# A two-block transformer on one core: where the experts' side work stands, and how the routing's slots are counted

## The chip, the cores and the metric

The kernel runs on one core of one Trainium2 chip. The metric is device time in microseconds of one execution; the median of several runs is compared. The engines' names are those of the profile: PE is TensorE (the matmuls), PEld its weight loads, DVE VectorE, ACT ScalarE, POOL GpSimd, SP the engine that issues most transfers.

## The reference

512 tokens of width 1024 go through two layers of a first block (four branches, a mixture of experts, a gated embedding) and two layers of a second one (three attentions). All is float32. The change touches the norms and the mixture of experts:

```python
def rms_norm(x, g):
    y = xf * lax.rsqrt(jnp.mean(xf * xf, axis=-1, keepdims=True) + EPS)

def expert_choice_moe(h, w_router, w_gate_e, w_up_e, w_down_e):
    cap = EC_CAPACITY * s // N_EXPERTS                      # 64 tokens for each of 16 experts
    affinity = jax.nn.softmax((h @ w_router).astype(jnp.float32), axis=-1)
    top_aff, idx = lax.top_k(jnp.swapaxes(affinity, 1, 2), cap)
    xe = h[bidx, idx]
    hid = silu(xe @ w_gate_e) * (xe @ w_up_e)               # 64 x 1024 by 1024 x 1024, per expert
    ye = hid @ w_down_e
    return jnp.zeros_like(h).at[bidx, idx].add(ye * top_aff[..., None])
```

Each expert chooses its 64 tokens, so every expert has the same amount of work, and its three matrices (4 MB each) are read once a layer.

## The kernel before, in words

The state `x` lies feature-major: eight tiles `x[kt]` of 128 features by 512 tokens. Products with float32 weights are done in two ways. Most are three matmuls of split values (`mm3`, a high and a low part). The experts' are plain float32 matmuls, which the trace shows as two records each.

`mean_sq` (L286) makes the mean of squares of `x` per token: ScalarE squares the eight tiles, VectorE adds them up one after the other (`sqa`), and four matmuls with a column of 1/1024 turn the sum into one number per token (`ms`). Eight places use it with one sum, one (the second block's first norm) with two.

`moe` (L1051) runs once in each of the first block's layers. **Routing:** the router's logits (`rlg`, `rlt`), the affinities `aff` (tokens on the partitions), and their transposes `aft` (16 experts on the partitions, 512 tokens along them). VectorE copies them to `w`, and eight times takes the eight largest and replaces them by -1. What is below zero then is the expert's choice. A scan along the tokens counts the chosen ones, times the mask; four transposes (`slt`) bring the counts back to tokens on the partitions, and `slot` holds for each token and expert the token's place 1 to 64, or 0. Meanwhile TensorE turns `x` (`h2t`) and computes the modulation of the second block (`ada`).

**Experts:** 16 experts in eight pairs (`pr`, counted from 0 to 7), 24 weight blocks of 1 MB a pair, fetched by SP in the order of use. A pool of buffers lets about ten blocks be ahead (`RING`). Expert `j` of a pair has 64 tokens; its matmuls have 64 weight columns and write 64 of the 128 partitions, `j` = 0 the lower half and `j` = 1 the upper one, each with its own weight block:

```python
for k2 in range(4):
    ts = [take() for j in range(2)]
    for k in range(2):
        for fh in range(2):
            for j in range(2):
                self.mat(two[fh][j * 64:j * 64 + 64], e[:, j * 64:j * 64 + 64], ts[j](k, fh), ...)
    step()
```

This is one step, eight matmuls or 16 records. The gate product has four steps and the up product four (`eg`), then come `sg` = silu of the gate, `hd` = `sg` times up, the transposes `hdt` and their copies `ht`, for the two halves `fh` of the width, and the down product with four steps (`ey`).

**Side work** comes from a list, `side`, one entry after each step, and what is left after the last one. Its entries: `scatter`, which adds a finished pair's results to one tile of `x` (two matmuls of 128x512 into `sct`, then an add on VectorE), eight for each pair, done during the next; `turned`, which transposes the pair's one-hot columns (`oht`) and picks the chosen affinities (`asl`); `gather`, which collects the tokens of four later experts (16 matmuls of 128x256 into `xe`, evicted half by VectorE, half by ScalarE), four in pair 1 and two each in pairs 2 to 5 (`GATHER`). The next stage's products `late` (a turn, eight parts `pw` of six matmuls, a load, two splits) come one after each step from pair 6 on, beside the list. All of the side work writes banks of the pool `at`, of which there are two.

The program only says what depends on what and in which order it was written; the framework lays out each engine's instructions. It goes by program order as a priority, and takes a later instruction where an earlier one isn't ready by its own estimate. So an engine's order in the trace need not be the program's: a gather can stand in two pieces around matmuls of the experts.

Of the kernel before, what the change touches and what calls it, by code (L numbers as in the profile page):

```python
# [10 lines left out]
FT = mybir.dt.float32  # L11
FR = mybir.dt.float32r
AF = mybir.ActivationFunctionType
OP = mybir.AluOpType
# [4 lines left out]
KT = 8  # L19
NB = 4  # L20
P = 128
# [67 lines left out]
class Net:  # L89
# [195 lines left out]

    def mean_sq(self, gains=(None,), on=None):  # L286

        acc = [None] * len(gains)
        pool = self.tr if len(gains) == 1 else self.ae
        for kt in range(KT):  # L290
            for i, g in enumerate(gains):
                sq = pool("sq")
                if g is None:
                    self.act(sq, self.x[kt], AF.Square)
                else:
                    self.act(sq, self.x[kt], AF.Square, scale=g[:, kt:kt + 1])
                if acc[i] is None:
                    acc[i] = sq
                else:
                    nx = pool("sqa")  # L300
                    (on or self.nc.vector).tensor_tensor(nx, acc[i], sq, op=OP.add)
                    acc[i] = nx
        ps = self.at("ms")
        for i in range(len(gains)):
            for tb in range(NB):
                self.mat(ps[:, i * NB + tb:i * NB + tb + 1], acc[i][:, tb * P:tb * P + P], self.inv1024)
        return [ps[:, i * NB:i * NB + NB] for i in range(len(gains))]

    def rms_cols(self, on=None):
# [741 lines left out]
    def moe(self, l, fill, late):  # L1051

        nc, ap = self.nc, self.ap
# [6 lines left out]
        def load():  # L1060
            to = plan.pop(0) if plan else "wst"
            src, k2 = order.pop(0)

            src = src.rearrange("(c p k) n -> c p k n", p=P, k=2)[k2]
            if to in ("fm", "tr", "ae"):
                t = [getattr(self, to)("we") for _ in range(4)]
                for k in range(2):
                    for h in range(2):
                        nc.sync.dma_start(t[k * 2 + h], src[:, k, h * S:h * S + S])
                ready.append(lambda k, h: t[k * 2 + h])  # L1070
            elif to == "wh":
                t = [self.sb.tile([P, 1024], FT, name="we" + y, tag=y, bufs=2) for y in ("wh", "wl")]
                for k in range(2):
                    nc.sync.dma_start(t[k], src[:, k])
                ready.append(lambda k, h: t[k][:, h * S:h * S + S])
            else:
                if to == "pt":
                    t = self.pt("we").rearrange("p a b -> p (a b)").rearrange("p (k n) -> p k n", k=2)
                elif to == "x":
                    if not half:  # L1080
                        for y in ("xh", "xl"):
                            big = self.sb.tile([P, 2, 2, D], FT, name="we" + y, tag=y, bufs=1)
                            half.extend((big[:, 0], big[:, 1]))
                    t = half.pop(0)
                else:
                    t = self.sb.tile([P, 2048], FT, name="wst", tag="wst", bufs=NW).rearrange("p (k n) -> p k n", k=2)
                nc.sync.dma_start(t, src)
                ready.append(lambda k, h: t[:, k, h * S:h * S + S])
# [46 lines left out]
        at = self.at("aft")  # L1135
        for tb in range(NB):
            self.tp(at[:16, tb * P:tb * P + P], afv[:, tb])
        w, cs = self.ae("rw"), self.ae("rcs")
        nc.vector.tensor_copy(w[:16], at[:16])
        for r in range(8):  # L1140
            m8 = self.sm("m8", 8)
            nc.vector.max(m8[:16], w[:16])
            nc.vector.match_replace(w[:16], m8[:16], w[:16], -1.0)
        ms = w
        self.ts(ms[:16], w[:16], 0.0, OP.is_lt)
        nc.vector.tensor_tensor_scan(cs[:16], ms[:16], ms[:16], 0.0, op0=OP.add, op1=OP.bypass)
        self.tt(cs[:16], cs[:16], ms[:16], OP.mult)

        hh = self.sb.tile([P, NB, 2, S], FR, name="h2h", tag="xl", bufs=1)
        hl = self.sb.tile([P, NB, 2, S], FR, name="h2l", tag="xh", bufs=1)  # L1150
        for hf in range(2):
            for tb in range(NB):
                ps = self.lgp("h2t")
# [6 lines left out]
        fill()  # L1160
        for _ in range(2):
            load()
        st = self.at("slt")
        for tb in range(NB):
            self.tp(st[:, tb * 16:tb * 16 + 16], cs[:16, tb * P:tb * P + P])
        slot = self.sb.tile([P, 64], FT, name="slot", tag="slot", bufs=1)
        nc.vector.tensor_copy(slot, st[:, :64])

        oh = [self.pt("oh%d" % hx, FR) for hx in range(2)]

# [28 lines left out]
        def turned(pr, out):  # L1199

            hx, cols = pr // 4, slice(pr % 4 * P, pr % 4 * P + P)
            ps = self.at("oht")
            for tb in range(NB):
                self.tp(ps[:, tb * P:tb * P + P], oh[hx][:, tb, cols].bitcast(FT))
            oht = self.ae("oht", FR)
            self.act(oht, ps, AF.Copy)
            pa = self.at("asl")
            for tb in range(NB):
                self.mat(pa[:, :2], oh[hx][:, tb, cols].bitcast(FT), afv[:, tb, pr * 2:pr * 2 + 2], start=tb == 0, stop=tb == NB - 1)
            asl = self.sm("asl", 1)  # L1210
            for j in range(2):
                nc.vector.tensor_copy(asl[j * 64:j * 64 + 64], pa[j * 64:j * 64 + 64, j:j + 1])
            out.extend((oht, asl))
# [5 lines left out]
            self.mat(ps, yl[:, c], oht, start=False, stop=True)  # L1219
            self.tt(self.x[i], self.x[i], ps, OP.add)  # L1220

        side = []

        def step():
            if side:
                side.pop(0)()
            if late and pr >= 6:
                late.pop(0)()
        xs, nxt = [], []
        onehot(0)  # L1230
        for pr in range(8):
            tn = []
            g4, part = GATHER.get(pr, (0, ()))
            if part and part[0] == 0:
                onehot(g4)
                nxt = []
            side.append(lambda pr=pr, tn=tn: turned(pr, tn))
            for d2 in part:
                side.append(lambda g4=g4, d2=d2, nx=nxt: gather(g4, d2, nx))
            xc = pr % 2 * P  # L1240
            pss = []
            for pool in (self.mm, self.lgp):
                two = [pool("eg%d" % i) for i in range(2)]
                for k2 in range(4):
                    ts = [take() for j in range(2)]
                    if pr == 0 and pool == self.mm:
                        gather(0, k2, xs)
                    for k in range(2):
                        kt = k2 * 2 + k
                        e = xs[kt // 2][:, kt % 2 * 256 + xc:kt % 2 * 256 + xc + P]  # L1250
                        for fh in range(2):
                            for j in range(2):
                                self.mat(two[fh][j * 64:j * 64 + 64], e[:, j * 64:j * 64 + 64],
                                         ts[j](k, fh), start=kt == 0, stop=kt == KT - 1)
                    step()
                pss.append(two)
            hts = []
            for fh in range(2):
                sg, hd = self.ae("sg"), self.ae("hd")
                self.act(sg, pss[0][fh], AF.Silu)  # L1260
                self.tt(hd, sg, pss[1][fh], OP.mult)
                pt = self.at("hdt")
                for k in range(4):
                    self.tp(pt[:, k * P:k * P + P], hd[:, k // 2 * 256 + k % 2:k // 2 * 256 + 256:2])
                ht = self.ae("ht")
                self.copy(ht, pt)
                hts.append(ht)
            py = [self.mm("ey%d" % i) for i in range(2)]
# [3 lines that stand above are left out]
                    ft = k2 * 2 + k  # L1272
                    for dh in range(2):
                        for j in range(2):
                            self.mat(py[dh][j * 64:j * 64 + 64], hts[ft // 4][:, ft % 4 * P + j * 64:ft % 4 * P + j * 64 + 64],
                                     ts[j](k, dh), start=ft == 0, stop=ft == KT - 1)
                step()
            while side:
                step()
            for dh in range(2):  # L1280
                yh, yl = self.tr("yh", FR), self.tr("yl", FR)
                self.split(yh, yl, py[dh], tn[1])
                for d in range(4):
                    side.append(lambda i=dh * 4 + d, yh=yh, yl=yl, oht=tn[0]: scatter(i, yh, yl, oht))
            if pr % 2:
                xs = nxt
        while side or late:
            step()

    def ple_pre(self, l):  # L1290

# [473 lines left out]
```

## Time and profile before

| | us |
|---|---|
| median of 3 runs | 3566.06 |
| lowest and highest | 3564.95, 3567.53 |
| the profiled execution, its own time | 3565.2 |
| span of the profile | 3563.5 |
| PE busy | 3430.4 |
| DVE busy | 1806.6 |
| ACT busy | 1133.5 |

The span goes from the first to the last instruction. A matmul counts as busy from its start to its modelled end, and neighbours overlap, so busy time does not tell how densely the array works; that is read from the distance of starts in the timeline. In the tables by stretch the columns are: from and to, the length, then for PE, PEld, DVE, ACT and POOL the busy time with the number of instructions, and last the granted clock of PE, the busy share of the transfer engines and the GB/s they moved. In a timeline the first two numbers are the start and the length; in square brackets stands the idle time before and what ended it.

The transfers moved 655.97 MB, 181 GB/s over the span, most of it in the two stages with the experts.

### The profile page before, as it was taken

Reading aid. Unit: us, or ns where it says so; the run is one execution under the profiler, and the core shown is the slowest. Engines: PE = TensorE matmul, PEld = TensorE weight load, DVE = VectorE, ACT = ScalarE, POOL = GpSimd, SP = SyncE. Lnnn points to the kernel's source line nnn. Section 1 sums busy time; section 2 is a strip of 40 time slices with the busy share of each in tenths; the row PEclk is TensorE's granted clock in tenths of the full one; section 3 lists DMA queues with packets and bytes.
Section 4 is the critical chain, followed back from the end, with each engine's and each line's share of the span. In section 5 each row is a group of like instructions: output and inputs, shape, how many; then the busy total and the mean of one; then the engine's idle time right before and its main releaser. Section 6 shows DMA issues by size and latency. Waiting matters only on the chain. (4 is left out here: it accounts for less than half of the span.)

```text
span 3563.5 us, 42081 instructions
## 1 busy us (share of the span) xinstructions
PE 3430.4 (96%) x15961; PEld 2298.0 (64%) x15961; DVE 1806.6 (51%) x3533; ACT 1133.5 (32%) x2209; POOL 419.1 (12%) x646
## 2 busy tenths in 40 slices
PE   8999999999999999999999999899999999999998
PEld 7867774443437877776434436676678877676887
DVE  7567652111117776673111115697644459756344
ACT  4344641000104444562000113225433322544333
POOL 0110421000000120151000000330210013103000
PEclk9999999999999999999999999899999999999999
DMA  5233667999993233465999985231123332221322
GB/s 177 73 88 108 199 216 282 385 387 388 376 378 109 66 111 105 149 231 202 388 373 402 380 353 226 71 101 62 46 76 103 102 116 76 79 71 36 107 95 71
DMA packets 315437, 655.97 MB, mean 184 GB/s; under 512 B 31075, under 2 KB 208575, under 8 KB 280931
## 3 DMA queue, kind: packets, MB, share of 16 engines
q1 hardware_dynamic: 291968, 628.78, 48.1%
q0 software_dynamic: 8192, 15.22, 1.7%
q10 hardware_dynamic: 15075, 9.29, 0.9%
q8 instruction: 126, 2.06, 0.2%
q14 instruction: 76, 0.62, 0.1%
HBM read 629.59 MB, written 14.70 MB: 181 GB/s over the span
## 5 line engine op out<-in xcount | busy, mean ns | idle before, releaser
L153 PE MATMUL pj<-xh,wh 128*128 128x512 f32 x1808 | 728.1, 404 | 14.3 <-DVE gb L150 6.4
L153 PE MATMUL pj<-xh,wl 128*128 128x512 f32 (+1 forms) x1808 | 725.1, 402 | 10.7 <-DVE wl L142 10.7
L153 PE MATMUL pj<-xl,wh 128*128 128x512 f32 (+1 forms) x1808 | 724.8, 401 | 0.9 <-DVE xl L150 0.7
L132 ACT ACTIVATE wh<-wst 128x1024 fp32r<-128x1024 f32 (+2 forms) x368 | 339.0, 930 | 754.2 <-PE pj L153 570.0
L142 DVE TENSOR_TENSOR wl<-wst,wh 128x1024 fp32r<-128x1024 f32 (+2 forms) x368 | 413.4, 1126 | 308.1 <-ACT wh L132 307.6
L153 PEld LDWEIGHTS pj<-xh,wh 128*128 128x128 f32 x1808 | 342.0, 189 | 110.0 <-DVE gb L150 9.6
L153 PEld LDWEIGHTS pj<-xh,wl 128*128 128x128 f32 (+1 forms) x1808 | 342.0, 189 | 102.7 <-DVE wl L142 13.7
L153 PEld LDWEIGHTS pj<-xl,wh 128*128 128x128 f32 (+1 forms) x1808 | 341.9, 189 | 94.2 <-issue 12.8
L153 PE MATMUL eg<-wst,xe 128*64 128x512 f32 x1008 | 293.0, 596 | 0.0
L153 PE MATMUL eg<-we,xe 128*64 128x512 f32 x560 | 228.4, 596 | 0.0
L153 PEld LDWEIGHTS eg<-wst,xe 128*64 128x64 f32 x1008 | 94.6, 136 | 134.1 <-issue 125.5
L142 DVE TENSOR_TENSOR x<-x,sct 128x512 f32<-128x512 f32 x128 | 83.8, 684 | 187.6 <-PE sct L153 187.6
L142 DVE TENSOR_TENSOR hd<-sg,eg 128x512 f32<-128x512 f32 x32 | 21.9, 685 | 309.0 <-PE eg L153 242.8
L153 PE MATMUL ey<-wst,ht 128*64 128x512 f32 x512 | 161.1, 599 | 7.4 <-DVE ht L139 3.9
L272 POOL TENSOR_TENSOR rr<-msb,mhalf 128x4 f32<-128x4 f32 x9 | 9.2, 1021 | 1344.9 <-DVE msb L146 1344.9
L153 PE MATMUL pt<-wh,xh 128*128 128x256 f32 x512 | 145.9, 285 | 1.4 <-DVE ro L142 1.2
L153 PE MATMUL pt<-wl,xh 128*128 128x256 f32 x512 | 145.1, 283 | 0.0
L153 PE MATMUL pt<-wh,xl 128*128 128x256 f32 x512 | 145.0, 284 | 0.0
L132 ACT ACTIVATE e<-e,nm 128x512 f32<-128x512 f32 (+3 forms) x192 | 111.2, 581 | 70.9 <-DVE nm L146 70.4
L1391 POOL TENSOR_TENSOR wada<-wada 128x1024 f32<-128x1024 f32 (+1 forms) x48 | 101.8, 2121 | 131.5 <-ACT wada L132 129.6
L153 PE MATMUL ey<-we,ht 128*64 128x512 f32 x256 | 115.3, 597 | 1.5 <-DVE ht L139 0.8
L153 PEld LDWEIGHTS eg<-we,xe 128*64 128x64 f32 x560 | 68.2, 136 | 74.2 <-issue 65.2
(495 smaller groups left out, 5788.9 us busy)
## 6 DMA issues: line engine op xcount, KB each, us to landing
wst<-in_w_in_dram SPq DMA_DIRECT2D x90, 1024.0 KB, 5.3
wst<-in_w_exp_gate_dram SPq DMA_DIRECT2D x66, 1024.0 KB, 8.6
wst<-in_w_exp_down_dram SPq DMA_DIRECT2D x64, 1024.0 KB, 11.1
wst<-in_w_exp_up_dram SPq DMA_DIRECT2D x60, 1024.0 KB, 7.8
wst<-in_w_branch_gate_dram SPq DMA_DIRECT2D x32, 1024.0 KB, 5.6
wada<-in_w_ada_dram SPq DMA_DIRECT2D x24, 1024.0 KB, 5.2
we<-in_w_exp_up_dram SPq DMA_DIRECT2D x88, 256.0 KB, 7.1
we<-in_w_exp_down_dram SPq DMA_DIRECT2D x80, 256.0 KB, 9.1
```

The lines of the kernel that those rows point to most:

```text
L132: return self.nc.scalar.activation(out, in_, func, **kw)
L142: return self.nc.vector.tensor_tensor(out, a, b, op=op)
L153: return self.nc.tensor.matmul(out, lhsT, rhs, start=start, stop=stop, **kw)
L272: self.nc.gpsimd.tensor_tensor(r, ms, self.mhalf[:, :n], op=OP.pow)
L1391: nc.gpsimd.tensor_tensor(t[:, :k], t[:, :k], t[:, k:2 * k], op=OP.add)
```

## The change

- In `mean_sq` the last square is no longer added: the sum of the first seven and the eighth square both go through the four matmuls, which add up in the bank.
- In the routing VectorE takes the first maxima straight from the transposes' bank. What is left after the eight rounds is transposed at once; the mask is taken there (64 columns), and the count is four matmuls: one with a triangle of ones within each block of 128 tokens, three with all ones that add the blocks before. A product with the mask gives `slot`.
- The list `side` becomes two: `sc`, scatters two at a time, and `ga`, gathers. Scatters stand after the first and third step of the gate and up products; `late` after the second and fourth. A gather stands before each `hd` (two where the pair has four), one after the last step of the down product, and what is left after it. `turned` has a fixed place after the second step of the down product.

```diff
@@ -285,7 +285,7 @@
 
     def mean_sq(self, gains=(None,), on=None):
 
-        acc = [None] * len(gains)
+        acc, last = [None] * len(gains), []
         pool = self.tr if len(gains) == 1 else self.ae
         for kt in range(KT):
             for i, g in enumerate(gains):
@@ -294,16 +294,21 @@
                     self.act(sq, self.x[kt], AF.Square)
                 else:
                     self.act(sq, self.x[kt], AF.Square, scale=g[:, kt:kt + 1])
-                if acc[i] is None:
+                if kt == KT - 1:
+                    last.append(sq)
+                elif acc[i] is None:
                     acc[i] = sq
                 else:
                     nx = pool("sqa")
                     (on or self.nc.vector).tensor_tensor(nx, acc[i], sq, op=OP.add)
                     acc[i] = nx
+
         ps = self.at("ms")
-        for i in range(len(gains)):
-            for tb in range(NB):
-                self.mat(ps[:, i * NB + tb:i * NB + tb + 1], acc[i][:, tb * P:tb * P + P], self.inv1024)
+        for src in (acc, last):
+            for i in range(len(gains)):
+                for tb in range(NB):
+                    self.mat(ps[:, i * NB + tb:i * NB + tb + 1], src[i][:, tb * P:tb * P + P], self.inv1024,
+                             start=src is acc and i + tb == 0, stop=src is last, skip_group_check=True)
         return [ps[:, i * NB:i * NB + NB] for i in range(len(gains))]
 
     def rms_cols(self, on=None):
@@ -1135,16 +1140,13 @@
         at = self.at("aft")
         for tb in range(NB):
             self.tp(at[:16, tb * P:tb * P + P], afv[:, tb])
-        w, cs = self.ae("rw"), self.ae("rcs")
-        nc.vector.tensor_copy(w[:16], at[:16])
+        w = self.ae("rw")
+        src = at
         for r in range(8):
             m8 = self.sm("m8", 8)
-            nc.vector.max(m8[:16], w[:16])
-            nc.vector.match_replace(w[:16], m8[:16], w[:16], -1.0)
-        ms = w
-        self.ts(ms[:16], w[:16], 0.0, OP.is_lt)
-        nc.vector.tensor_tensor_scan(cs[:16], ms[:16], ms[:16], 0.0, op0=OP.add, op1=OP.bypass)
-        self.tt(cs[:16], cs[:16], ms[:16], OP.mult)
+            nc.vector.max(m8[:16], src[:16])
+            nc.vector.match_replace(w[:16], m8[:16], src[:16], -1.0)
+            src = w
 
         hh = self.sb.tile([P, NB, 2, S], FR, name="h2h", tag="xl", bufs=1)
         hl = self.sb.tile([P, NB, 2, S], FR, name="h2l", tag="xh", bufs=1)
@@ -1160,11 +1162,20 @@
         fill()
         for _ in range(2):
             load()
+
         st = self.at("slt")
         for tb in range(NB):
-            self.tp(st[:, tb * 16:tb * 16 + 16], cs[:16, tb * P:tb * P + P])
+            self.tp(st[:, tb * 16:tb * 16 + 16], w[:16, tb * P:tb * P + P])
+        ms = self.sb.tile([P, 64], FT, name="chosen", tag="chosen", bufs=1)
+        self.ts(ms, st[:, :64], 0.0, OP.is_lt)
+        cn = self.at("cnt")
+        self.mat(cn[:, :64], self.tri[:, 0], ms, start=True, stop=False, skip_group_check=True)
+        for tb in range(1, NB):
+            self.mat(cn[:, tb * 16:64].rearrange("p (b e) -> p b e", e=16), self.one.to_broadcast([P, P]),
+                     ms[:, None, tb * 16 - 16:tb * 16].to_broadcast([P, NB - tb, 16]), start=False, stop=tb == NB - 1,
+                     skip_group_check=True)
         slot = self.sb.tile([P, 64], FT, name="slot", tag="slot", bufs=1)
-        nc.vector.tensor_copy(slot, st[:, :64])
+        self.tt(slot, cn[:, :64], ms, OP.mult)
 
         oh = [self.pt("oh%d" % hx, FR) for hx in range(2)]
 
@@ -1219,12 +1230,16 @@
             self.mat(ps, yl[:, c], oht, start=False, stop=True)
             self.tt(self.x[i], self.x[i], ps, OP.add)
 
-        side = []
-
-        def step():
-            if side:
-                side.pop(0)()
-            if late and pr >= 6:
+
+
+        sc, ga = [], []
+
+        def step(kind):
+            if kind == 0 and sc:
+                sc.pop(0)()
+            elif kind == 1 and ga:
+                ga.pop(0)()
+            elif late and pr >= 6:
                 late.pop(0)()
         xs, nxt = [], []
         onehot(0)
@@ -1234,9 +1249,8 @@
             if part and part[0] == 0:
                 onehot(g4)
                 nxt = []
-            side.append(lambda pr=pr, tn=tn: turned(pr, tn))
             for d2 in part:
-                side.append(lambda g4=g4, d2=d2, nx=nxt: gather(g4, d2, nx))
+                ga.append(lambda g4=g4, d2=d2, nx=nxt: gather(g4, d2, nx))
             xc = pr % 2 * P
             pss = []
             for pool in (self.mm, self.lgp):
@@ -1252,12 +1266,15 @@
                             for j in range(2):
                                 self.mat(two[fh][j * 64:j * 64 + 64], e[:, j * 64:j * 64 + 64],
                                          ts[j](k, fh), start=kt == 0, stop=kt == KT - 1)
-                    step()
+                    step(k2 % 2 * 2)
                 pss.append(two)
             hts = []
             for fh in range(2):
                 sg, hd = self.ae("sg"), self.ae("hd")
                 self.act(sg, pss[0][fh], AF.Silu)
+                step(1)
+                if len(part) == 4:
+                    step(1)
                 self.tt(hd, sg, pss[1][fh], OP.mult)
                 pt = self.at("hdt")
                 for k in range(4):
@@ -1274,18 +1291,21 @@
                         for j in range(2):
                             self.mat(py[dh][j * 64:j * 64 + 64], hts[ft // 4][:, ft % 4 * P + j * 64:ft % 4 * P + j * 64 + 64],
                                      ts[j](k, dh), start=ft == 0, stop=ft == KT - 1)
-                step()
-            while side:
-                step()
+                if k2 == 1:
+                    turned(pr, tn)
+                elif k2 == 3:
+                    step(1)
+            while ga:
+                step(1)
             for dh in range(2):
                 yh, yl = self.tr("yh", FR), self.tr("yl", FR)
                 self.split(yh, yl, py[dh], tn[1])
-                for d in range(4):
-                    side.append(lambda i=dh * 4 + d, yh=yh, yl=yl, oht=tn[0]: scatter(i, yh, yl, oht))
+                for d in (0, 2):
+                    sc.append(lambda i=dh * 4 + d, yh=yh, yl=yl, oht=tn[0]: [scatter(i + j, yh, yl, oht) for j in range(2)])
             if pr % 2:
                 xs = nxt
-        while side or late:
-            step()
+        while sc or late:
+            step(0)
 
     def ple_pre(self, l):
 
```

## Rows read from the trace of the kernel before

**Rows 1.** The page's first part: busy time, share of the span, instructions.

```profile
PE 3430.4 (96%) x15961; PEld 2298.0 (64%) x15961; DVE 1806.6 (51%) x3533; ACT 1133.5 (32%) x2209; POOL 419.1 (12%) x646
```

**Rows 2.** Busy time of each engine over the first layer's experts.

```profile
556.56:1077.04 520.48, 506.31 (x2125) 217.02 (x2125) 88.67 (x150) 52.49 (x87) 0.31 (x1) 1.00 0.95 375
```

**Rows 3.** The same view for `eg` alone, twice, and for `ey` alone.

```profile
694.20:715.05 20.85, 20.85 (x96) 8.61 (x96) 0.69 (x1) 0.60 (x1) 1.00 0.99 389
...
556.56:1077.04 520.48, 258.20 (x1024) 92.51 (x1024) 11.00 (x16) 9.51 (x16) 1.00 0.95 375
...
556.56:1077.04 520.48, 141.53 (x512) 43.93 (x512) 11.90 (x16) 10.90 (x16) 1.00 0.95 375
```

**Rows 4.** Timeline of PE in pair 1: start, length, engine, what, count, idle before.

```profile
613.22 0.50 PE L153 MATMUL sct<-oht,yh 128*128 128x512 f32 x1
...
613.88 3.65 PE L153 MATMUL eg<-wst,xe 128*64 128x512 f32 x16
617.46 0.50 PE L153 MATMUL sct<-oht,yh 128*128 128x512 f32 x1
...
622.37 1.93 PE L153 MATMUL eg<-we,xe 128*64 128x512 f32 x4
...
628.57 0.40 PE L153 MATMUL sct<-oht,yh 128*128 128x512 f32 x1
628.80 0.39 PE L153 MATMUL sct<-oht,yl 128*128 128x512 f32 x1
```

**Rows 5.** Timeline of PE in pair 2, the start of the down product.

```profile
716.48 1.93 PE L153 MATMUL ey<-wst,ht 128*64 128x512 f32 x4 [0.69 <-ACT ht L137]
718.34 0.75 PE L157 MATMUL hdt<-ident,hd 128*128 128x128 f32 x4
718.92 0.60 PE L157 MATMUL oht<-ident,oh 128*128 128x128 f32 x4
...
720.85 3.65 PE L153 MATMUL ey<-wst,ht 128*64 128x512 f32 x12
...
724.67 0.28 PE L153 MATMUL xe<-oh,h2l 128*128 128x256 f32 x1
724.79 0.28 PE L153 MATMUL xe<-oh,h2h 128*128 128x256 f32 x1
```

**Rows 6.** Waits of PE: who was waited for, us in total, times, longest.

```profile
PE slt L157 <- DVE rcs L142: 13.9, 2, 6.9
...
PE ms L153 <- DVE sqa L301: 7.6, 2, 4.8
```

**Rows 7.** Down parts (five summed, the last pair's); gate and up parts (seven summed).

```profile
sum 139.26, PE 133.68 PEld 64.56 DVE 17.16 ACT 17.60 POOL 0.00; mean PE 26.74 PEld 12.91 DVE 3.43 ACT 3.52 POOL 0.00
...
1050.07:1069.74 19.67, 18.64 (x85) 8.16 (x84) 1.72 (x5) 2.37 (x4) 0.00 (x0) 1.00 1.04 399
...
sum 280.26, PE 275.25 PEld 104.56 DVE 54.98 ACT 16.62 POOL 0.31; mean PE 39.32 PEld 14.94 DVE 7.85 ACT 2.37 POOL 0.04
```

**Rows 8.** Stretches of the experts; the last two numbers: DMA share, GB/s.

```profile
640.00:655.00 15.00, 13.97 (x63) 6.11 (x61) 4.02 (x10) 1.68 (x3) 0.00 (x0) 1.00 1.02 423
...
609.00:936.00 327.00, 317.62 (x1335) 132.86 (x1332) 54.20 (x96) 24.59 (x44) 0.00 (x0) 1.00 0.99 388
```

**Rows 9.** Timeline of DVE in the routing.

```profile
535.09 0.68 DVE L1139 COPY rw<-aft 16x512 f32<-16x512 f32 x1 [0.78 <-PE aft L157]
...
547.74 0.76 DVE L146 TENSOR_SCALAR rw<-rw 16x512 f32<-16x512 f32 x1
548.54 1.21 DVE L1146 TENSOR_TENSOR_SCAN rcs<-rw 16x512 f32<-16x512 f32 x1
549.79 0.68 DVE L142 TENSOR_TENSOR rcs<-rcs,rw 16x512 f32<-16x512 f32 x1
551.23 0.22 DVE L1167 COPY slot<-slt 128x64 f32<-128x64 f32 x1 [0.76 <-PE slt L157]
```

**Rows 10.** Timeline of PE at the second block's second norm.

```profile
2895.63 1.02 PE L153 MATMUL ms<-inv,sqa 128*128 128x1 f32 x8 [2.74 <-DVE sqa L301]
```

## The prediction, made before the changed kernel ran

> **What bounds the kernel now.** First the head of the page: TensorE is busy for 3430.4 us, 96% of the span [rows 1]. So time comes off only where TensorE's own work gets shorter, or where it waits with everybody behind it. Next the stage table, cut where the experts' matmuls begin and end: one layer's experts take 520.5 us, TensorE is busy through 506 of it and the transfers run at 375 GB/s [rows 2]. The second layer shows the same pattern, so I work out one layer and double it.
>
> Then I asked what a busy TensorE does there. In an undisturbed run 96 records of the gate and up matmuls take 20.85 us, 0.217 each [rows 3]. A pair of experts has 128 such records (two products, 8 row blocks, two halves of the width, two experts, two records per matmul) and 64 more in its down product, so a layer has 1536, which at 0.217 would take 333 us. The trace has 258.2 for `eg` and 141.5 for `ey` [rows 3]: 66 us a layer are lost inside "busy". The timeline says to what [rows 4, 5]:
> - Going out of the half-width matmuls and back. One step of 16 records with its scatter takes 4.24 us (613.22 to 617.46); 16 x 0.217 and two scatter matmuls at 0.23 (628.57 to 628.80) are 3.93. A break costs 0.31.
> - A step cut in two. A run of 4 records lasts 1.86 us to the next instruction (716.48 to 718.34), 0.465 a record: twice the undisturbed time, so I read it as one expert's half of the columns working alone. Its other 12 need 3.58 (720.85 to the gather that follows it, whose second record is at 724.67), as much as a whole undisturbed step (613.88 to 617.46). Each cut costs 1.86, on top of the break. The cuts lie where side work was taken in: a run of 4, transposes and `turned`, a run of 12, then a gather [rows 5].
>
> Last, the wait at the routing: TensorE stands still for 13.9 us in two waits until VectorE has the slots [rows 6].
>
> **The change, part by part.**
>
> *Gathers out of the down product.* Five pairs a layer gather for later ones (one pair four times, four pairs twice). Their down parts, from the first transpose of `hd` to the next pair, take 139.3 us together [rows 7]. Without side work but for the one `turned` in the middle, such a part is 64 x 0.217 = 13.9, two groups of four transposes at 0.58 (718.34 to 718.92) with a break, 1.5, and `turned` at no more than the 1.93 from 718.92 to 720.85. A gather is 16 records at 0.12 (724.67 to 724.79) and some 0.2 of entry, 2.1 [rows 5]. That gives 21.5 with two gathers and 25.7 with four, 111.7 for the five: 27.6 less. In this the 0.69 that `ey` waits for the copy of `ht` is gone as well [rows 5], since a gather fills it. What hides what: the gathers run while ScalarE and VectorE make `sg`, `hd` and `ht`. Behind them wait the transposes, which need one of the two `at` banks, so where two gathers stand together the first one's eviction must come ahead of them; with one gather the other bank is free. The bounds are 0 (the cuts come back elsewhere) and 27.6. I take all of it, since a down part with hardly any gather in it is short already: the last pair's takes 19.7 [rows 7].
>
> *Scatters two at a time, on every second step.* The gate and up parts of the seven pairs that scatter take 280.3 us [rows 7], with the next stage's `late` work in one of them. In program order each would be 128 x 0.217 = 27.8 and four runs of two scatters (4 x 0.23 + 0.31 = 1.23): 32.7, 229 for seven. The `late` work, eight parts of six matmuls at 0.23 with a break each, is some 14 of the rest: up to 37 to win. But the instructions don't stand in program order today: eight scatters that the program spreads over eight steps are done in the first five or six of their pair, and cut steps on their way, as at 622.37 [rows 4]. Where a scatter is taken early whenever a weight block isn't counted on yet, a new place in the program hardly moves it: bound below 0. The row nearest is that one, so I take 8 of 37.
>
> *Weights.* A layer's experts are 16 x 3 matrices of 4.19 MB, 201.3 MB. In 520.5 - 27.6 - 8 = 485 us the same transfers mean 375 x 520.5 / 485 = 402 GB/s. Over five pairs the queue brings 388 with its engines 0.99 busy, and 423 in the best of some 15 us stretches [rows 8]. So faster matmuls come close to what the transfers give, and what is late next is a weight block. I charge 4 us a layer; the bounds are 0 and, at 388 throughout, 375 x 520.5 / 388 = 503, which would leave 17 of the gain.
>
> On this the Trainium skill, "DMA: Bandwidth & Descriptors", section Specifications, speaks against the change: about 358 GB/s from HBM for one core. By that figure the layer's 188 MB that are left after 13 blocks fetched ahead take 524 us, and the experts gain nothing. The rows at 388 and 423 are already above it, so the measurement decides here.
>
> *`late` work.* Its last two items, the load of the next stage's first weights and their splits, move from the seventh pair to the eighth's up product, and SP sends the load behind more weight blocks. I cost it at nothing: the eighth's down part, 19.7 us [rows 7], lies ahead of its user. Without that cover it would be 1 MB at 388 GB/s, 2.7 us a layer. `turned` moves a few steps; its result is needed at the end of the down product, half a down part later. No instruction of POOL's queue moves.
>
> *Routing.* Off VectorE's chain go the copy 0.68, the compare 0.76, the scan 1.21 and the product 0.68: 3.33 [rows 9]. In come a compare and a product on 128x64 (0.22 each, one of them in place of the slot copy), one crossing to TensorE and back, and four small matmuls, eight records. The nearest is `ms`, eight records in 1.02 [rows 10]; these come after an idle stretch like it. With crossings of 0.1 to 0.4 the chain gets 1.0 to 2.0 shorter; I take 1.4 a layer, all of it gain, because TensorE idles there.
>
> *Norms.* The last add leaves the chain, an operation as long as the 0.68 of the same width in [rows 9], and eight more records come, as long as the eight of `ms`, 1.02 [rows 10]. Where TensorE waits for the add (twice, 7.6 us in all [rows 6]) and at the very end some 0.7 is gained, with the running sum's records standing in the wait; at the other six places the add was hidden and the records aren't, up to 1.0 lost each, against a chain that is 0.7 earlier. I take 0, bounds 4 either way.
>
> **Sum.** 27.6 + 8 - 4 = 31.6 a layer, 63 for two; routing 2.8; norms 0: 66 us. The profiled execution took 3565.2, so 3499; the median shown is 0.9 above it: 3500.
>
> **The rivals.**
> 1. *The transfers decide.* If 388 GB/s is what the mix of block sizes gives, each layer keeps 17.4 us: 3565.2 - 34.8 - 2.8 + 0.9 = 3528. For it: engines 0.99 busy at 388; against it: the stretch at 423. Chance 0.20. The page's 358 would be its extreme: only routing is left, 3563; with both rows above it I give that 0.01, inside rival 3.
> 2. *Program order holds everywhere.* 27.6 + 37 is more than the transfers allow: at 423 GB/s the stage can't be under 461 us, 59 less a layer: 3566 - 118 - 3 = 3445. Against it: today's order. Chance 0.12.
> 3. *The change doesn't do what it says.* The order on TensorE stays one of readiness, gathers fall into the down product as before, and only routing is left: 3563. For it: the cut steps of today. Against it: the gathers' new place is ahead of the transposes in program order, at a moment when TensorE has nothing else. Chance 0.09.
> 4. *Slower: more cut steps.* Longer runs of side work, some of it waiting from the start of a pair, get into the middle of steps. A cut and its break cost 2.2; the 66 us lost today are at most some 30 cuts a layer. From 14 more on (31.6 / 2.2) the change loses; with 21 more it is 14 us a layer: 3590. Chance 0.11.
>
> **How the numbers follow.** My forecast has 0.48, with a range of its own of 3475 to 3522 (the scatters' 0 to 20, the transfers' 0 to 10). A measurement of this kernel tells some 0.2%, 7 us, from no change. Faster: forecast, rivals 1 and 2, 0.80; same: rival 3, 0.09; slower: rival 4, 0.11. The range for 8 in 10 runs from rival 2 to the edge of "same": 3445 to 3558.
>
> **What would show it.** In the profile after: the five down parts together near 112, with `ey` in two runs of 32 and `xe` ahead of and between the `hdt` groups; `eg` and `ey` together well under 400 a layer; `sct` in runs of four, and fewer runs of 4 and 12; transfers above 400 GB/s over the same five pairs, and whether TensorE now names a weight transfer as what it waited for; the wait for `slt` near 5.5 each. I am wrong if `ey` still comes in runs of 4 and 12, or if waits for `we` and `wst` add up to tens of us.

## The result, and the profile after

The changed kernel takes 3520.62 us (median of 4 runs, 3519.08 to 3526.85), the kernel before beside it 3565.51: ratio 0.9877, 95% interval 0.986 to 0.9894, 44.9 us less. The forecast was 3500: right side and inside the range, but of the 66 us that it promised a third did not come.

The head of the page of the changed kernel [rows 1]:

```profile
PE 3408.0 (97%) x16057; PEld 2309.6 (66%) x16057; DVE 1794.9 (51%) x3517; ACT 1133.6 (32%) x2209; POOL 417.3 (12%) x646
```

TensorE is busy for 22.4 us less. The stage table over the experts of both layers, then the first layer's `eg` and its `ey` alone [rows 2, 3]:

```profile
560.91:1062.12 501.21, 491.64 (x2123) 215.62 (x2123) 88.42 (x150) 52.00 (x86) 0.31 (x1) 1.00 0.98 390
1643.85:2139.57 495.72, 486.69 (x2123) 215.06 (x2123) 87.69 (x150) 51.98 (x86) 0.00 (x0) 1.00 0.98 393
...
560.91:1062.12 501.21, 259.13 (x1024) 93.15 (x1024) 10.99 (x16) 9.52 (x16) 1.00 0.98 390
...
560.91:1062.12 501.21, 127.84 (x512) 42.54 (x512) 11.91 (x16) 10.89 (x16) 1.00 0.98 390
```

The first layer's experts are 19.3 us shorter, the second's 26.8 (522.5 before): 46 us, the whole gain. `ey` lost 13.7 of its busy time; `eg` nothing.

The parts of the first layer: the five down parts that had gathers in them, summed, then the gate and up parts of the seven pairs with scatters, summed [rows 7]:

```profile
sum 105.20, PE 104.44 PEld 50.47 DVE 14.16 ACT 14.74 POOL 0.00; mean PE 20.89 PEld 10.09 DVE 2.83 ACT 2.95 POOL 0.00
...
sum 293.85, PE 287.59 PEld 116.52 DVE 60.10 ACT 20.22 POOL 0.31; mean PE 41.08 PEld 16.65 DVE 8.59 ACT 2.89 POOL 0.04
```

The down parts are 34.1 us shorter, and the gate and up parts, forecast 8 shorter, are 13.6 longer. Neither can be read by itself. The parts meet at the first transpose of `hd`, and six of a layer's gathers, which the program now puts before the first `hd` of their pair, have crossed that border; the forecast counted all twelve in the down parts. Busy time of TensorE in the same seven gate and up parts: all instructions that use `xe`, which are the gathers and `eg`; `eg` alone; and, in the kernel before, `eg` alone, since no gather stood there:

```profile
sum 293.85, PE 242.55; mean PE 34.65
...
sum 293.85, PE 229.56; mean PE 32.79
...
sum 280.26, PE 228.71; mean PE 32.67
```

The six gathers are 13.0 of the 13.6 us. Counted as the forecast counts, the down parts gave 21.1 us of its 27.6, and the gate and up parts are 0.6 longer, with one part of `late`, some 1.7 us, gone from them (in pairs 6 and 7, where no gather is left, `late` takes the gathers' places too). Of runs of 4 records, the sign of a cut step, the first layer's `eg` has 16 before and 16 after, its `ey` 13 before and 1 after. So the cut steps left the down product and stayed as they were in the gate and up products. How they come about is in the timeline of TensorE in pair 3:

```profile
739.71 1.93 PE L153 MATMUL eg<-wewh,xe 128*64 128x512 f32 x4
741.57 0.73 PE L153 MATMUL sct<-oht,yl 128*128 128x512 f32 x2
742.84 0.50 PE L153 MATMUL sct<-oht,yh 128*128 128x512 f32 x1 [0.54 <-DVE x L142]
...
746.86 1.88 PE L153 MATMUL eg<-we,xe 128*64 128x512 f32 x4
748.67 0.50 PE L153 MATMUL sct<-oht,yh 128*128 128x512 f32 x1
...
750.17 0.49 PE L153 MATMUL sct<-oht,yh 128*128 128x512 f32 x1 [0.33 <-DVE x L142]
750.60 1.93 PE L153 MATMUL eg<-wst,xe 128*64 128x512 f32 x4
752.46 0.50 PE L153 MATMUL sct<-oht,yl 128*128 128x512 f32 x1
752.80 0.28 PE L153 MATMUL xe<-oh,h2h 128*128 128x256 f32 x1
...
753.97 3.65 PE L153 MATMUL eg<-wst,xe 128*64 128x512 f32 x12
```

A cut step begins with 4 records of one half alone (739.71, from `wewh`) and ends with 4 of the other half alone (746.86, from `we`), 1.9 us each, with scatters in between that the program puts after later steps. All eight scatters of the pair are through by 752.8; one of them, at 750.17 and 752.46, is itself cut in two. At 752.80 a gather, which stands behind the up product in the program, follows after 20 of the pair's 128 `eg` records, in the middle of a step. I read the runs of 4 as one half of a step that goes alone because the other's weight block isn't there yet in the framework's reckoning, with side work taken in its place; the halved transfers below test it.

The waits of TensorE at the two places [rows 6]:

```profile
PE slt L157 <- DVE rw L1148: 6.1, 2, 3.7
...
PE ms L153 <- ACT sq L132: 3.1, 2, 2.3
```

The routing's wait fell from 13.9 to 6.1. What stands behind it now (TensorE, from the routing to the first gather):

```profile
552.24 0.58 PE L157 MATMUL slt<-ident,rw 16*128 16x16 f32 x4 [3.75 <-DVE rw L1148]
553.23 0.66 PE L153 MATMUL cnt<-chosen,pc 128*128 128x64 f32 x2 [0.41 <-DVE chosen L146]
553.68 1.41 PE L153 MATMUL cnt<-chosen,one 128*128 128x48 f32 x6
555.95 0.55 PE L153 MATMUL xe<-oh,h2h 128*128 128x256 f32 x1 [0.87 <-DVE oh L1185]
```

From `slt` to the first gather it is 3.71 us, before 1.44: 2.27 of the 3.2 that the wait lost in this layer (6.94 before) are given back.

### The profile page after: what moved, and what is told of

The parts are those of the page before. It is cut to its first block, busy times and chain, and to the rows that moved or that the text cites. A ratio compares the mean times of both kernels' runs of the same rounds, so it can differ in the third digit from the quotient of the medians.

```text
span 3518.1 us, 42207 instructions
## 1 busy us (share of the span) xinstructions
PE 3408.0 (97%) x16057; PEld 2309.6 (66%) x16057; DVE 1794.9 (51%) x3517; ACT 1133.6 (32%) x2209; POOL 417.3 (12%) x646
## 5 line engine op out<-in xcount | busy, mean ns | idle before, releaser
L153 PEld LDWEIGHTS pj<-xh,wl 128*128 128x128 f32 (+1 forms) x1808 | 342.1, 189 | 102.9 <-DVE wl L142 13.9
L153 PE MATMUL ey<-wst,ht 128*64 128x512 f32 x512 | 145.1, 596 | 2.9 <-DVE ht L139 1.6
```

The costliest lines, as they stand in the source:

```text
L153: return self.nc.tensor.matmul(out, lhsT, rhs, start=start, stop=stop, **kw)
```

## Experiments

The excess below is, for a layer's `eg` and `ey`, the time from the start of each run to the next instruction, less 0.2145 a record (329.5 us; in an undisturbed run two records, one of each half, start every 0.43 us): breaks, cut steps and waits inside steps together. It is 65.6 and 66.1 us in the two layers before, 54.9 and 51.0 after. The runs were made in three groups, each beside its own runs of the kernel before (3564.59, 3567.45 and 3564.55), so times from different groups compare to some 3 us.

### The three parts one by one

```diff
 (experts alone)
+        sc, ga = [], []
...
+                    step(k2 % 2 * 2)
 (routing alone)
+        self.mat(cn[:, :64], self.tri[:, 0], ms, start=True, stop=False, skip_group_check=True)
...
+        self.tt(slot, cn[:, :64], ms, OP.mult)
 (norms alone)
+                if kt == KT - 1:
+                    last.append(sq)
```

> The kernel before with the change of the experts' lists alone; norms and routing as before. Theory (the whole gain is the experts' stages): the two stages lose 46 us together as in the full change (520.5 to 501.2 and 522.5 to 495.7), so about 3519, within 4 us of the full change. Rival (the parts feed each other, the shorter routing above all): the experts alone give under 35 us, 3530 or more.

> The kernel before with the change of the routing alone. Theory (the wait for slt shortens by 3 to 4.5 us a layer, and the four count matmuls with their crossing, 2.7 us at the lower clock, take that back): within 2 us of before, 3563 to 3567. Rival (the prediction's term, 1.4 us a layer, stands): 3562 to 3563. Both are near what the rounds can tell apart; the stretch from rlg to the first eg tells more: 28.8 before; theory 28.5 to 29.2, rival 27.4.

> The kernel before with the norms' change alone. Theory (the eight more records are bare in the first block, and the place of the last add is worth something only where TensorE waited for it): in the profile the first layer's router comes about 4 us later, the second block wins 1 to 3 us; total 0 to 4 us slower, 3565 to 3570. Rival (the late start of the full change has another cause): the router's start stays within 1 us, the total is 1 to 4 us faster.

Measured beside 3564.59 for the kernel before: experts alone 3515.82 (ratio 0.985 to 0.9877), routing alone 3562.95 (0.9986 to 1.0004), norms alone 3570.34 (1.0006 to 1.0024). So -48.8, -1.6 and +5.7; their sum, -44.7, is the full change. The gain is the experts': alone they come 4.8 us under the full change, where within 4 had been expected. The routing can't be told from nothing in the times. In its profile, counted from `rlg`, `slt` comes 2.3 and 3.0 us earlier in the two layers, but the first `eg` comes 1.2 later and 0.5 earlier: 30.3 and 28.6 us behind `rlg`, where the trace before has 29.1 in both layers (not 28.8). The norms lose, more than the theory's 0 to 4, and the first layer's router starts 1.6 us later, not 4. Their profile gains 2 us in the second block and loses 8 up to there, over half of it at the norm ahead of the routing, 2.1 and 2.3 us between `rlg` and `slt`. TensorE there, before and with the norms' change alone, and last VectorE's scan with it:

```profile
527.42 1.92 PE L153 MATMUL rlg<-x,wrz 128*32 128x512 f32 x16
529.28 0.55 PE L157 MATMUL h2t<-ident,x 128*128 128x128 f32 x3
529.81 1.02 PE L153 MATMUL ms<-inv,sqa 128*128 128x1 f32 x8
...
531.06 0.96 PE L153 MATMUL rlt<-sel,rlf 128*128 128x16 f32 x8
...
534.45 0.60 PE L157 MATMUL aft<-ident,aff 128*16 128x128 f32 x4 [0.30 <-DVE aff L142]
```

```profile
529.04 1.92 PE L153 MATMUL rlg<-x,wrz 128*32 128x512 f32 x16
530.90 1.05 PE L153 MATMUL ms<-inv,sqa 128*128 128x1 f32 x8
531.81 1.03 PE L153 MATMUL ms<-inv,sq 128*128 128x1 f32 x8
...
533.28 0.96 PE L153 MATMUL rlt<-sel,rlf 128*128 128x16 f32 x8
534.10 3.18 PE L157 MATMUL h2t<-ident,x 128*128 128x128 f32 x15
537.07 0.96 PE L157 MATMUL aft<-ident,aff 128*16 128x128 f32 x4
...
551.35 2.16 DVE L1151 TENSOR_TENSOR_SCAN rcs<-rw 16x512 f32<-16x512 f32 x1
```

`rlg` and three transposes covered the last add before; now a second run of eight records stands in the chain, and `rlt` comes 4.24 us after `rlg` in place of 3.64. Ahead of `aft` stand 20 of the turn's transposes in both kernels, but from 534.10 to 537.07 TensorE's granted clock is 0.55, where it was 1.00 before, and `aft` comes 8.03 us after `rlg` in place of 7.03. Most of the other 1.1 us is the scan, which takes 2.16 us in place of 1.21 [rows 9]. It takes 2.16 with the experts' change alone as well, so the norms' records by themselves aren't the cause; the cause stays open. In the full change there is no scan, so that the three parts add up to 0.2 us is partly chance.

### The written order, held

```diff
     def mat(self, out, lhsT, rhs, start=True, stop=True, **kw):
-        return self.nc.tensor.matmul(out, lhsT, rhs, start=start, stop=stop, **kw)
+        ins = self.nc.tensor.matmul(out, lhsT, rhs, start=start, stop=stop, **kw)
+        return self.tc.keep_in_program_order(ins) if self.pin else ins
```

The same for transposes; `pin` is set from the experts' first matmul to the last scatter.

> The full change, with TensorE's instructions of the experts held in the order in which they are written (an order on one engine's queue, no wait added). Theory (what the change left on the table is cut steps: 55 and 51 us a layer in eg and ey, because side work is taken where a weight block isn't counted on yet): the excess of eg and ey falls under 20 us a layer, gate and up parts go from about 41 to 34 us; then the transfers come into view at 400 to 423 GB/s: 3440 to 3490. Rival (the transfers already set the pace of the changed kernel): the cut steps go and waits for weight blocks of the same size take their place: 3510 to 3525. Second rival (an order without regard to what is ready stalls at the start of pairs, on yh and on the at banks): over 3530.

Measured: 3496.18, ratio 0.9799 to 0.9825 to before, 24 us under the change. The stage table by pair, pairs 1 to 5 of the first layer, first of the change, then in the held order:

```profile
614.22:678.54 64.32, 63.62 (x295) 28.62 (x291) 13.66 (x28) 5.64 (x11) 0.00 (x0) 1.00 1.02 404
678.54:739.04 60.50, 59.08 (x261) 25.04 (x260) 9.97 (x18) 4.65 (x9) 0.00 (x0) 1.00 0.97 386
739.04:799.98 60.94, 59.78 (x260) 25.65 (x260) 9.99 (x18) 4.44 (x8) 0.00 (x0) 1.00 1.00 393
799.98:860.37 60.39, 59.62 (x262) 25.60 (x261) 9.97 (x18) 4.60 (x8) 0.00 (x0) 1.00 1.01 397
860.37:922.78 62.41, 61.23 (x262) 26.36 (x261) 9.98 (x18) 4.61 (x8) 0.00 (x0) 1.00 1.01 405
```

```profile
610.49:668.59 58.10, 57.41 (x294) 26.06 (x292) 13.62 (x27) 5.49 (x11) 0.00 (x0) 1.00 1.03 415
668.59:724.89 56.30, 54.47 (x263) 22.59 (x260) 9.98 (x17) 4.47 (x9) 0.00 (x0) 1.00 1.02 411
724.89:785.94 61.05, 57.58 (x262) 25.13 (x260) 9.99 (x17) 4.51 (x9) 0.00 (x0) 1.00 1.02 414
785.94:846.95 61.01, 57.25 (x262) 25.95 (x260) 9.99 (x17) 4.46 (x9) 0.00 (x0) 1.00 1.02 401
846.95:913.59 66.64, 59.89 (x262) 26.41 (x261) 9.98 (x17) 4.52 (x9) 0.00 (x0) 0.95 1.01 405
```

Pairs 1 and 2 win 10.4 us, and TensorE waits for no weight there before 697 us: the cut steps of the change were not needed in them. Pairs 3 to 5 are 5.0 longer, 4.2 of it in pair 5; pairs 6 and 7 win 11.8 (139.3 to 127.6), pair 0 loses 2.3. TensorE now names weights, as in these rows of its waits over the whole run, the longest of them in pair 5, and a stretch right behind that one:

```profile
PE eg L153 <- DMA we<-in_w_exp_up_dram: 10.6, 6, 3.5
...
PE eg L153 <- DMA wst<-in_w_exp_up_dram: 4.8, 4, 1.2
...
881.02 1.12 PE L153 MATMUL eg<-we,xe 128*64 128x512 f32 x1 [3.53 <-DMA we<-in_w_exp_up_dram]
...
882.00:884.00 2.00, 2.00 (x8) 0.65 (x6) 0.00 (x0) 0.00 (x0) 0.00 (x0) 0.50 1.01 426
```

This wait costs more than its 3.53 us. TensorE has nothing to do in it and goes on at a granted clock of 0.50, with two records every 0.86 us in place of 0.43, until about 887 us.

Theory and first rival hold each in a stretch, and the time is between their ranges. The excess fell to 42 and 44 only, where under 20 had been expected, since a step in which one half waits for its block counts into it.

### The transfers halved

Both experts of a pair are given the first one's weight blocks; the second one's aren't read.

```diff
-                 for k2 in range(4) for j in range(2)]
+                 for k2 in range(4) for j in range(1)]
...
-                    ts = [take() for j in range(2)]
+                    ts = [take()] * 2
```

> The full change, TensorE's order left to readiness, with half the weight transfers: both experts of a pair are given the first one's weight blocks, so the second ones' blocks aren't read and the results are others. Theory (side work is taken early where a weight block isn't counted on yet, so the cut steps go when the blocks come twice as early): the excess of eg and ey over 0.2145 a record falls from 55 and 51 us a layer to under 20, gate and up parts of pairs 2 to 5 near 34 us, time within 10 us of the kernel with half the transfers and the written order. Rival (the cuts come from what the side work itself waits for): the excess stays over 40 us.

> As the run before this one (half the weight transfers, other results), with TensorE's instructions of the experts held in the order in which they are written. Theory (in that order with all transfers, 3496 us, the weight blocks set the pace from the third pair on): no waits for weights, all eg and ey runs of 32 near 7.02 us, a layer's experts 440 to 450 us in place of 486 to 488: 3405 to 3425. Rival (TensorE's own work sets it): within 15 us of 3496.

> The kernel before with half the weight transfers (the second expert of a pair is given the first one's blocks; other results), order by readiness. Theory (the cut steps of the kernel before come from weight blocks that aren't counted on yet, the old places cost only breaks and waits for ht by themselves): the excess of eg and ey falls from 66 to about 30 us a layer, 3445 to 3470. Rival (the old list makes cut steps by itself): excess over 50 us a layer, 3500 or more.

Measured, a single run each: 3421.61 for the change in its own order, 3424.49 in the held one, 3453.39 for the kernel before. The stage of the first layer in the three:

```profile
555.25:1007.82 452.57, 449.39 (x2123) 192.15 (x2123) 88.62 (x151) 51.59 (x86) 0.31 (x1) 1.00 0.60 209
```

```profile
557.66:1012.51 454.85, 444.03 (x2128) 186.88 (x2129) 88.61 (x151) 52.00 (x87) 0.31 (x1) 1.00 0.59 208
```

```profile
554.93:1022.70 467.77, 464.06 (x2124) 190.84 (x2125) 91.14 (x151) 52.50 (x87) 0.31 (x1) 1.00 0.57 203
```

With half the bytes the excess is 17.5 in the change's own order, with no run of 4 records of `eg` left, and 9 to 11 in the held one, and the two take the same time. So the cut steps are not the side work's: they come and go with when the weights are there, or are reckoned to be. One thing these runs don't separate: the two halves of a step now use one block, so neither can be there without the other, whatever the bytes. The price of the full transfers, block shortage and all, is 501.2 - 452.6 = 48.6 us in this layer in the change's own order, and 486 - 455 = 31 in the held one, with the stretch at the lower clock in pair 5 included. The kernel before, with its old places, gets 520.5 - 467.8 = 52.7 us shorter by the same halving. And what the new places are worth to TensorE by themselves, without a shortage of weights, is 467.8 - 452.6 = 15.2 us (13.3 in the second layer). The held order's layers, 454.9 and 452.5, are a little over the 440 to 450 expected.

### The kernel before, in its written order

The same edit of `mat` and of the transposes on the kernel before.

> The kernel before, nothing of the change, with TensorE's instructions of the experts held in the order in which they are written. Theory (most of what the change moves is cut steps, which a held order takes away wherever the side work stands; what is left of the old places is breaks, 28 more of 0.31, and waits for ht, 0.69 each, some 20 us a layer, of which the waits for weight blocks hide most): 3492 to 3510. Rival (the places count by themselves, the order adds to it): 3525 or more, less than half of the gap to 3496 closed.

Measured: 3501.58 (0.9804 to 0.9834), as the theory has it. Nothing of the change is in it, and it is 19 us faster than the change. The old places cost TensorE breaks and waits:

```profile
PE hdt L158 <- DVE hd L142: 27.1, 16, 2.0
```

The held order of the change with the norms of the second block alone, from the same group (below), is 12.7 us faster than this kernel. Without a shortage of weights the new places were worth 28.5 in two layers, so the transfers seem to hide more than half of that.

### Gathers alone, scatters alone

```diff
 (gathers at the new places, scatters one a step)
-            if kind == 0 and sc:
+            if kind in (0, 2) and sc:
...
 (scatters in pairs, gathers one after each step of the down product)
-                step(1)
-                if len(part) == 4:
-                    step(1)
...
-                elif k2 == 3:
+                else:
                     step(1)
```

> The full change (3520.6), but scatters again one after each step of gate and up, as before; gathers at their new places; order by readiness. Beside it the norms and the routing alone come to 3569 (before plus 5.7 minus 1.6). Theory (in an order by readiness the pairing of the scatters does next to nothing; the gathers' places carry the gain): within 8 us of the full change, 3513 to 3529. Rival (the pairing carries a third or more of the 48): 3537 or more.

> The full change, but with the gathers again one after each step of the down product (turned at its new place); scatters in pairs; order by readiness. Theory (the pairing does next to nothing): within 8 us of 3569. Rival (the pairing carries a third or more): 3553 or less.

Measured: 3524.04 (0.9875 to 0.9902) and 3559.03 (0.9976 to 0.9994). Without the pairing the change loses 3.4 us in two layers, inside the intervals of both. Without the gathers' places it loses 38. The second kernel misses the theory's 3561 by 2: against 3569 it has 10 us, 7 more than the pairing is worth beside the new gathers. It has `turned` and `late` at their new places too; which of them it is wasn't separated.

### Towards a faster version

```diff
 (norms' change in the second block alone, with the held order)
+    n.two = True
     n.begin2()
 (and no block in four small tiles)
-RING = ["pt"] + ["wst"] * 5 + ["fm"] * 2 + ["wh"] * 2
+RING = ["pt"] + ["wst"] * 5 + ["wh"] * 2
```

> The full change in the written order, with the norms' change in the second block and the final norm alone, where TensorE waits for the sum of squares; the first block's norms as before. Theory (the norms' change alone cost 8 us up to the end of the first block and won 2 us behind it): 5 to 9 us under the 3496 of the written order, 3487 to 3491. Rival (what the first block lost is the framework's other arrangement of the whole list, not those records): within 3 us of 3496.

> The written order with the norms' change in the second block alone (3488.9), and in the steady part of a layer no block in the four small tiles (2 KB a packet): eight blocks ahead in place of ten. In the trace of the former, from 700 to 1000 us, 8 KB packets move at 423 GB/s (16 engines), 4 KB ones at 378 and 2 KB ones at 384. Theory (the transfers set the pace and the size of a packet sets their rate): 1.7% more GB/s, 8 us a layer less, 3470 to 3480. Rival (the number of blocks ahead counts for more, with two fewer each is fetched later than its buffer's turn allows): 3489 or more.

Measured: 3488.85 (0.9766 to 0.9799), 7.3 under the held order with all norms; and 3474.70 (0.9745 to 0.9772), 14.2 less again. Stretches of 300 us of the two, the first layer's; the last number is GB/s:

```profile
700.00:1000.00 300.00, 286.22 (x1288) 128.22 (x1290) 50.47 (x84) 29.29 (x50) 0.31 (x1) 0.99 1.01 412
```

```profile
700.00:1000.00 300.00, 288.81 (x1314) 129.16 (x1312) 53.81 (x88) 31.28 (x52) 0.31 (x1) 1.00 1.01 423
```

Larger packets, 423 GB/s, with two blocks fewer ahead. The last kernel is the best of the study, 90 us under the kernel before.

## Why the prediction was right, and where it was wrong

- **The loss it read was there, but most of it did not hang on the places.** With the weights early, a layer of the changed kernel takes 452 to 455 us, and the forecast's terms for TensorE at their full size, 27.6 and 37, give 520.5 - 64.6 = 456. But halving the transfers takes 52.7 us off the kernel before with its places as they were; the new places add 15.2. The price of a cut step was sound; that new places take the cuts away held in the down product alone.
- **Gathers, 27.6.** Mechanism right in the down product: `ey` lost 13.7 us of busy time, and its runs of 4 are gone but for one. Counted with all gathers the gain is 21.1. The forecast's part began at the first transpose of `hd` and yet held the gather that stands ahead of it, so the 34.1 of the bare part is not its term. One of a pair's gathers, or part of it, went to the middle of the gate and up product, where the program does not put it.
- **Scatters, 8 of 37.** Nothing came of them: beside the gathers the gate and up parts are 0.6 longer. Pairing alone is worth 3.4 us in both layers, not 16. The row at 622.37 had been read rightly (side work is taken early), and its own bound, 0, was the better figure; the same holds for every gather that is ready.
- **Transfers, 4: the term that was furthest off.** It was worked out from GB/s, as a wait. The halved transfers put it at 48.6 us in the first layer in the change's own order, 37 of it in the excess of `eg` and `ey`: TensorE names no weight block among its larger waits in the changed kernel, for the order fills such waits with side work. In the held order it is 31, and pairs 3 to 5 are no faster there. Rival 1 had the mechanism, and its 503 us a layer is nearer to the 501.2 measured in the first layer than the forecast's 489, and as near to the second's 495.7; its rate did not hold: the same mix of blocks went at 407 GB/s in the held order. The total, 3520.62, lies at the edge of the forecast's own range and 7 us from rival 1's 3528, so the number alone doesn't choose between them.
- **Its signs.** `ey` in runs of 4 and 12 and waits for weights would have shown it wrong: hardly any of the first, none of the second. But the transfers stayed at 397 GB/s, under the 400 it named, and the scatters did not come in runs of four throughout.
- **Routing, 1.4 a layer.** -1.6 us in both together, inside the noise: the chain is shorter, but the count's eight records took 1.86 us (553.23 to 555.09), where they were costed at the 1.02 of `ms`. TensorE's granted clock is 0.50 from 552.2 to 555.9, its level of 1.2 GHz.
- **Norms, 0 with 4 either way.** +5.7, outside the bounds. The records were counted. Not counted were the second run's place in the router's chain, the granted clock of 0.55 behind it, and the scan's 2.16 us.

By parts: 48.8 of the 63 forecast for the experts, 1.6 of 2.8, and -5.7 of 0: 44.7 in place of 66.

## What to carry to other kernels

Where a framework orders an engine's queue by what it reckons to be ready, a new place in the program is a wish: look first whether the instructions of the trace stand where the program has them, and try the written order held before moving anything, for here that alone, a few lines, gave more (66 us beside its own runs of the kernel before) than the change (45). Such an order also shows the next limit by name, because TensorE then waits instead of filling in. And halve a suspected resource in one run: it prices the resource and TensorE's own work at once. Mind what else the halving changes: here both halves of a step came to share one block.

## What the runs showed of the hardware

A DMA share of 1.0 isn't a ceiling of GB/s. Over pairs 1 to 5 the same mix of blocks went at 388 GB/s before at a share of 0.99 [rows 8], at 397 after at 1.00, at 407 in the held order, and at 422 without the blocks in small tiles, the last two over 608 to 900 us. By each packet's own duration in the trace of the held order with the second block's norms (700 to 1000 us), 16 engines move 8 KB packets at 423 GB/s, 2 KB ones at 384 and 4 KB ones at 378. But without the 2 KB packets the 4 KB ones go at 411, so the size alone doesn't set the rate; what slows packets that share the engines with small ones stays open. In the kernel before, over the same 300 us, the 8 KB packets themselves went at 409: the share counts a packet's time as busy however long it takes. The Trainium skill, "DMA: Bandwidth & Descriptors", section Specifications, gives 512 B as enough for line rate; in this mix packets of 2 KB are 9% slower than those of 8 KB, and the measurement decides for it. How fast 2 KB packets go by themselves no run shows. The same section's 358 GB/s from HBM for a core is passed by each of these stretches.
